# First norm from a token-major copy of x, first weights by halves, and a new order of the early pairs

## The chip, the cores and the metric

The kernel runs on one core of one Trainium2 chip. The metric is the device time of one execution, in microseconds (us). The engines are TensorE (PE), VectorE (DVE), ScalarE (ACT), GpSimd (POOL) and SyncE (SP), which here issues transfers. Each engine works through its own queue in order; semaphores tie the queues together.

## The reference

Two groups of requests, 512 and 256 tokens of 1024 features, go through two layers with shared weights. Cut to what matters:

```python
def rmsnorm(x, g):
    y = x32 * lax.rsqrt(jnp.mean(x32 * x32, axis=-1, keepdims=True) + EPS)
    return y.astype(x.dtype) * g

def swiglu(h, wg, wu, wd):
    return (jax.nn.silu(h @ wg) * (h @ wu)) @ wd

def even_layer(x, ...):
    x = x + 0.5 * swiglu(rmsnorm(x, f1_n), f1_g, f1_u, f1_d)
    x = x + mixer_ab(rmsnorm(x, mix_n), ...)
    x = x + 0.5 * swiglu(rmsnorm(x, f2_n), f2_g, f2_u, f2_d)
    return x
```

The odd layer is the same with `mixer_c` in the middle, and a last rmsnorm follows. The inner width of swiglu is 2816. All is float32.

## The kernel before, in words

**Phases.** The kernel runs l0f1, l0m, l0f2, l1f1, l1m, l1f2 (layer 0 and 1: first swiglu, mixer, second swiglu). x lies in SBUF feature-major, as 8 tiles of 128 features by 768 tokens; the tokens are cut into two halves of 384 columns (`HALVES`, `H` = 384).

**Products.** A float32 operand is split into a high part, rounded to fp32r (`...h`, `whi`), and the rest (`...l`, `wlo`). ACT makes the high part (`copy`, or an activation with the gain as its scale), DVE the low part by a subtraction. `mm3` then issues three fp32r matmuls: weights high by data high, weights high by data low, weights low by data high.

**One pair.** The inner width is worked in 11 pairs of 256 columns. For each pair, gate and up are computed by seven block products in place of eight, over blocks of x (feature half by token half) and blocks of the weights, with sums of blocks: `p1` (on b11, tiles x0 to x3 of the first token half), `p2` (on b21, x4 to x7 of the first half), then `p6` (t2), `p7` (t3), `p4` (n4), `p5` (t1) and `p3` (b22). t2, t3, t1 and n4 are sums of blocks of x, made with DVE combines (`tmp<-x,gains,tmp`). One block product is 12 matmuls of 128x128 by 384 columns. p1 and p2 of gate and up are 24 matmuls each.

**Early pairs.** For the first four pairs (`EARLY`) p1, p2 and the activation (`hidden(0, 0)`) run before anything else, in the order of the tuple `ORDER`; each number is the next step of that pair. They need only the first token half. p1 leaves its result in a PSUM bank, and ACT copies it to SBUF (`p`, L524) before p2 adds to the same bank. `product` takes a bank from one of two pools of four, `mm` and `aux`; in before, pair 3's bank X is in aux, the others' in mm. The weights come as `raw` tiles of 128x1024 (512 KB), four buffers; the five `whi` and five `wlo` buffers rotate.

**Norm.** The gain is multiplied in when the high and low parts are made; 1/rms, a number per token, is multiplied in behind the matmuls, in `hidden` (L508, L510). For a token half ACT squares the eight tiles (L216, L219), DVE sums them into `acc` (L220), three matmuls of `acc` by ones give the sums per token (`norm_tok`), a chain of 12 small DVE operations makes rsqrt, and `norm_spread` makes two diagonal matrices, of the high and the low part (`diag`, DVE L256 and ACT L254), which two matmuls by ones spread over all partitions. ACT copies the result to `acc` (L414). `hidden(0, 0)` needs that copy for the first half.

**Order.** PE's order is the order of the code (`manual_schedule`). The code of the norm and of the splits runs in generators (chains) that yield planned us: `DELAY0` sets how many planned us of PE's work lie ahead of the sum and of the spread for the first token half, and so where their matmuls stand in PE's queue. The order on the other engines is set by a scheduler, which `high_priority` and `issue_after` guide. SP issues its transfers in order, with up to eight in flight: each waits for the eighth before it. At the start they are x0 to x3 (first token half), two raws, x4 to x7, two raws, the second half of x, and the raws of pairs 2 and 3. Transfers for the later tables (`skew`) are put between raws.

## Time and profile before

| what | value |
|---|---|
| time, median of 3 runs | 2619.56 us (2619.34 to 2621.04) |
| time of the profiled execution | 2622.39 us |
| its span, first to last instruction | 2620.6 us |
| mean granted clock of PE | 0.991 |
| PE busy | 2559.6 us (98%) |
| DVE busy | 2257.1 us (86%) |
| ACT busy | 1369.9 us (52%) |
| first matmul | 9.11 us after the span's start |

Rows of the timeline give the start in us from the span's start, the length, the engine, the line, the operation, its tiles (out<-in) and its shape; brackets hold the idle time before it and what ended it. Neighbouring rows of an engine overlap a little, so what one costs is the distance of the starts. "ps_mm" and "ps_aux" are the two pools of PSUM. PE's matmuls are named by the data and the weights that they read: `ps_mm<-b110h,whi` is a matmul of p1.

### The profile page before, as it was taken

The numbers are of one execution on the slowest core, as the hardware profiler recorded it, in microseconds if no ns is written. First come the engines' busy times: TensorE is split into PE (matmuls) and PEld (weight loads), VectorE is DVE, ScalarE is ACT, GpSimd is POOL, SyncE is SP. The second block draws the span as 40 slices with busy tenths as digits, with TensorE's granted clock in tenths as the row PEclk, the third lists the DMA queues.
The fourth block names the chain that finished last, engine by engine and source line by source line (L and its number), as shares of the span: only waits on it lengthen the run. The fifth ranks groups of instructions, "written<-read, shape, count | busy, mean of one in ns | idle before, by whom it ended". The sixth has DMA issues, their size and how long they took to land.

```text
span 2620.6 us, 41173 instructions
## 1 busy us (share of the span) xinstructions
PE 2559.6 (98%) x15106; PEld 2493.7 (95%) x15106; DVE 2257.1 (86%) x4727; ACT 1369.9 (52%) x2858; POOL 90.4 (3%) x172
## 2 busy tenths in 40 slices
PE   7999999999999999999999999999999999999997
PEld 7999999988899999999999999989898999999997
DVE  8998899888779989889999888986777689888897
ACT  7554454555665545445654444554545465444543
POOL 0000000000100000000000000001122100000000
PEclk9999999999999999999999999999999999999999
DMA  5333222421222222222322222232221332222221
GB/s 169 114 110 97 80 66 65 156 73 45 81 77 97 97 74 72 75 79 73 98 80 89 73 66 80 81 115 60 63 63 42 104 102 85 81 71 75 73 69 69
DMA packets 83897, 218.72 MB, mean 83 GB/s; under 512 B 20208, under 2 KB 33008, under 8 KB 83696
## 3 DMA queue, kind: packets, MB, share of 16 engines
q1 hardware_dynamic: 83552, 216.08, 26.2%
q8 instruction: 118, 1.93, 0.3%
q14 instruction: 83, 0.68, 0.1%
q10 hardware_dynamic: 144, 0.03, 0.0%
HBM read 206.64 MB, written 15.07 MB: 85 GB/s over the span
## 4 chain that ended last, share of the span: by engine, by line
PE 86%; DVE 8%; ACT 3%; DMA 1%; issue 1%; POOL 0%; SPq 0%; DVEq 0%; ACTq 0%; POOLq 0%
PE ps_mm L140 54%; PE ps_aux L140 31%; DMA raw<-in_w 1%; DVE wlo L115 1%; PE ps_aux L144 1%; ACT p L913 1%; DVE xl L741 1%; DVE p L907 1%; DVE s L611 0%; DVE tl L197 0%; ACT whi L114 0%; DVE p L922 0%; ACT xh L740 0%; DVE x L708 0%; ACT sq L219 0%
## 5 line engine op out<-in xcount | busy, mean ns | idle before, releaser
L114 ACT CAST whi<-s 128x512 fp32r<-128x512 f32 x496 | 305.0, 620 | 409.6 <-DVE s L611 164.6
L114 ACT CAST whi<-raw 128x512 fp32r<-128x512 f32 x512 | 311.2, 618 | 238.0 <-PE ps_mm L140 104.2
L115 DVE TENSOR_TENSOR wlo<-s,whi 128x512 fp32r<-128x512 f32 x496 | 337.2, 685 | 55.5 <-ACT whi L114 53.2
L115 DVE TENSOR_TENSOR wlo<-raw,whi 128x512 fp32r<-128x512 f32 x494 | 336.7, 689 | 29.9 <-ACT whi L114 25.8
L140 PE MATMUL ps_mm<-db,whi 128*128 128x384 f32 x864 | 219.3, 334 | 0.5 <-DVE sg L508 0.5
L140 PE MATMUL ps_aux<-dt,whi 128*128 128x384 f32 x864 | 219.1, 334 | 0.0
L140 PEld LDWEIGHTS ps_mm<-db,whi 128*128 128x128 f32 x864 | 155.9, 188 | 0.8 <-DVE sg L508 0.8
L140 PEld LDWEIGHTS ps_aux<-dt,whi 128*128 128x128 f32 x864 | 156.0, 188 | 0.0
L140 PE MATMUL ps_mm<-xh,whi 128*128 128x512 f32 (+1 forms) x416 | 147.1, 354 | 4.0 <-ACT xh L740 4.0
L140 PE MATMUL ps_mm<-db,wlo 128*128 128x384 f32 x432 | 144.3, 334 | 0.0
L140 PE MATMUL ps_aux<-dt,wlo 128*128 128x384 f32 x432 | 144.3, 334 | 0.0
L140 PE MATMUL ps_mm<-xl,whi 128*128 128x512 f32 (+1 forms) x416 | 142.2, 342 | 1.1 <-DVE xl L741 1.1
L140 PE MATMUL ps_mm<-xh,wlo 128*128 128x512 f32 (+1 forms) x416 | 141.8, 341 | 0.0
L611 DVE TENSOR_TENSOR s<-raw 128x512 f32<-128x512 f32 x124 | 85.2, 687 | 23.7 <-DMA raw<-in_w 23.4
L611 DVE TENSOR_TENSOR s<-raw,raw 128x512 f32<-128x512 f32 x124 | 84.0, 686 | 21.1 <-DMA raw<-in_w 21.0
L499 DVE TENSOR_TENSOR u<-ps_aux,u 128x384 f32<-128x384 f32 x176 | 97.1, 552 | 3.9 <-PE ps_aux L140 3.5
L140 PE MATMUL ps_aux<-dh,whi 128*128 128x384 f32 x384 | 97.7, 335 | 0.6 <-DVE x L708 0.6
L913 ACT ACTIVATE p<-p,st 128x256 f32<-128x256 f32 (+3 forms) x144 | 68.9, 480 | 52.5 <-DVE st L911 52.4
L663 DVE TENSOR_TENSOR x<-ps_aux,x 128x384 f32<-128x384 f32 x160 | 84.8, 551 | 13.0 <-PE ps_aux L140 13.0
L140 PE MATMUL ps_mm<-oh,whi 128*128 128x384 f32 x256 | 89.6, 350 | 4.7 <-DVE x L890 4.0
L140 PEld LDWEIGHTS ps_mm<-xh,whi 128*128 128x128 f32 x416 | 80.3, 193 | 14.0 <-ACT xh L740 4.9
L140 PE MATMUL ps_mm<-ol,whi 128*128 128x384 f32 x256 | 87.9, 343 | 3.5 <-DVE ol L197 3.3
(488 smaller groups left out, 8049.3 us busy)
## 6 DMA issues: line engine op xcount, KB each, us to landing
raw<-in_w SPq DMA_DIRECT2D x350, 512.0 KB, 3.7
xdm<-x SPq DMA_DIRECT2D x16, 384.0 KB, 2.3
x<-in_x SPq DMA_DIRECT2D x16, 192.0 KB, 5.5
x<-xdm SPq DMA_DIRECT2D x8, 384.0 KB, 4.0
xold<-xdm SPq DMA_DIRECT2D x8, 384.0 KB, 3.0
out_y<-y SPq DMA_DIRECT2D x8, 384.0 KB, 2.4
tab<-skew SPq DMA_DIRECT2D x8, 256.0 KB, 5.5
raw<-in_w SPq DMA_DIRECT2D x8, 256.0 KB, 2.7
```

The costliest lines, as they stand in the source:

```text
L114: nc.scalar.copy(hi, src)
L115: (eng or nc.gpsimd).tensor_tensor(out=lo, in0=src, in1=hi.bitcast(F32), op=ALU.subtract)
L140: self.nc.tensor.matmul(out, lhsT=lhsT, rhs=rhs, start=start, stop=stop, **kw)
L144: self.nc.tensor.transpose(out, src, self.ident)
L499: nc.vector.tensor_tensor(out=t, in0=bank[key, n], in1=t, op=ALU.add)
L611: f = lambda o, x, y, op: self.nc.vector.tensor_tensor(out=o, in0=x, in1=y, op=op)
L663: nc.vector.tensor_tensor(out=o, in0=ps, in1=o, op=ALU.add)
L741: nc.vector.scalar_tensor_tensor(out=lo, in0=src, scalar=gain, in1=hi.bitcast(F32), op0=ALU.mult, op1=ALU.subtract)
L907: nc.vector.tensor_tensor_reduce(out=outs[i], in0=ps_list[i], in1=adds[i], scale=1.0, scalar=init[i], op0=ALU.add, op1=ALU.max, accum_out= ...
L913: nc.scalar.activation(outs[i], outs[i], AF.Exp, bias=nm[:, i : i + 1], accum_out=sm[:, i : i + 1])
```

## The change

In the first phase (l0f1) the sums of squares come from a second input, `xt`, x in token-major form (6 blocks of 128 tokens by 1024 features, 3.15 MB). It is loaded in 12 tiles of 128x512 (`tok_load`; eight buffers, the last four behind the first four squares). ACT squares each and sums along the row in the same instruction (`accum_out`); DVE adds the two halves and makes rsqrt for all 768 tokens in one chain of 6 columns. The diagonal matrices of the first half are made at once. The combines and splits of t3, n4, t1 and b22 are issued behind the last DVE piece of them (`rooted`). The squares stand behind the first two copies of p1, the second half of x behind the fourth.

The first weights are cut into halves of 256 KB: the first of them goes on ACT's queue, ahead of the gains, three behind x0 to x3, four behind x4 to x7. 22 matmuls of ones by ones (128 columns) stand ahead of the first product. POOL sets `ones` before `ident`.

In l0f1 and l1f1 (not in the phases that follow a mixer) the early pairs run in a new order: both steps of pair 2 before `hidden` of pairs 0 and 1. Pair 2's bank X is in aux there, pair 3's in mm. In these phases the second number of `DELAY0` is 13 in place of 11 (l0f1 has its own, `DELAYT`). `hidden(0, 0)` of l0f1 has high priority. The skew transfers begin four raws later.

SP's order at the start, before:
```order
1 L1459 DMA x_97<-in_x 128x384
2 L1459 DMA x_98<-in_x 128x384
3 L1459 DMA x_99<-in_x 128x384
4 L1459 DMA x_100<-in_x 128x384
5 L99 DMA raw_190<-in_w 128x1024
6 L99 DMA raw_192<-in_w 128x1024
7 L1459 DMA x_101<-in_x 128x384
```
and in the changed kernel (`first_87` to `first_90` are the weights of p1 and p2, gate and up of pair 0, then of pair 1):
```order
4 L1526 DMA x_106<-in_x 128x384
5 L104 DMA first_88<-in_w 128x512
6 L104 DMA first_89<-in_w 128x512
7 L104 DMA first_90<-in_w 128x512
8 L1526 DMA x_107<-in_x 128x384
9 L1526 DMA x_108<-in_x 128x384
10 L1526 DMA x_109<-in_x 128x384
11 L1526 DMA x_110<-in_x 128x384
12 L104 DMA first_87<-in_w 128x512
13 L104 DMA first_88<-in_w 128x512
14 L104 DMA first_89<-in_w 128x512
15 L104 DMA first_90<-in_w 128x512
```
The weights of p1 now stand as halves ahead of x4 to x7, those of p2 behind; behind these rows follow eight token tiles, then the second half of x, then the last four token tiles and the raws of pair 2. ACT's queue at the start, changed kernel:
```order
1 L104 DMA first_87<-in_w 128x512
2 L1504 ACT_TABLE_LOAD
3 L1504 COPY space<-ones 128x96
4 L1507 DMA gains<-in_gains 128x56
5 L119 CAST whi_257<-first_87 128x512
6 L399 ACTIVATE b110h<-x_103,gains 128x384
7 L119 CAST whi_276<-first_88 128x512
8 L399 ACTIVATE b111h<-x_104,gains 128x384
```
In before the gain rows of x0, x1 and x2 stood ahead of the first weight cast; now two casts stand among them.

ACT's queue later in l0f1, where before the copies p of pair 1 stand between splits:
```order
48 L196 CAST t22h<-tmp 128x384
49 L354 ACTIVATE t13h<-tmp,gains 128x384
50 L219 ACTIVATE sq<-x_104 128x384
51 L524 COPY p_343<-ps_mm_272 128x384
52 L196 CAST b221h<-tmp 128x384
53 L524 COPY p_385<-ps_mm_345 128x384
```
and in the changed kernel the copies p of pair 2 (those of pairs 0 and 1 stand further ahead, among the first squares):
```order
49 L119 CAST whi_618<-raw_593 128x512
50 L201 CAST b222h<-tmp 128x384
51 L296 ACTIVATE diag<-ident,yl 128x128 x2
52 L119 CAST whi_644<-raw_591 128x512
53 L296 ACTIVATE diag<-ident,yl 128x128
54 L201 CAST b223h<-tmp 128x384
55 L201 CAST t30h<-tmp 128x384
56 L201 CAST t31h<-tmp 128x384
57 L201 CAST t32h<-tmp 128x384
58 L569 COPY p_513<-ps_aux_492 128x384
59 L569 COPY p_535<-ps_aux_515 128x384
```
The copies that p2 of pair 2 needs now stand behind the diags and three casts of t3.

PE's queue at the start of l1f1, before (`ps_mm_13945` is the third block product, gate of pair 1):
```order
6811 L140 MATMUL ps_mm_13945<-b110h,whi_13946 128x384
6812 L140 MATMUL ps_mm_13945<-b110l,whi_13946 128x384
6813 L140 MATMUL ps_mm_13945<-b110h,wlo_13947 128x384
6814 L140 MATMUL ps_aux_13957<-diag,onesr 128x384 x2
6815 L140 MATMUL ps_mm_13945<-b111h,whi_13946 128x384
```
and in the changed kernel, where `ps_mm_13943` is that product and `ps_mm_13970` the one behind it:
```order
6820 L145 MATMUL ps_mm_13943<-b113h,whi_13944 128x384
6821 L145 MATMUL ps_mm_13943<-b113h,wlo_13945 128x384
6822 L145 MATMUL ps_mm_13970<-b110h,whi_13971 128x384
6823 L145 MATMUL ps_mm_13970<-b110l,whi_13971 128x384
6824 L145 MATMUL ps_mm_13970<-b110h,wlo_13972 128x384
6825 L145 MATMUL ps_aux_13990<-diag,onesr 128x384 x2
```
The spread of the norm stands one block product, 12 matmuls, further back.

The diff, cut to its core:

```diff
-DELAY0 = (7.0, 11.0)
+DELAY0 = (7.0, 13.0), (7.0, 11.0)
+WARM = 22
 DELAY1 = (26.0, 12.0)
+DELAYT = (0.0, 14.6)
+TOKW, TOKQ, SECOND = 2, (8, 0), 4
...
 EARLY = 4
-ORDER = (0, 1, 0, 1, 0, 2, 1, 3, 2, 3, 2, 3)
+ORDERS = (0, 1, 0, 1, 2, 2, 0, 1, 3, 2, 3, 3), (0, 1, 0, 1, 0, 2, 1, 3, 2, 3, 2, 3)
...
-        self.nc.sync.dma_start(raw, src)
-        if self.spare and i >= 16:
+        if raw is None:
+            raw = self.rawp.tile([P, nk * n], F32, tag="raw", name=f"raw{i}")
+        (eng or self.nc.sync).dma_start(raw, src)
+        if self.spare and i >= 20:
             self.spare.pop(0)()
...
+    def tok_load(self):
+
+        i = len(self.tok)
+        t = self.fw.tile([P, 512], F32, tag="s", name="tok", bufs=8)
+        self.nc.sync.dma_start(t, self.aps["xt"][i // 2, :, i % 2 * 512 : i % 2 * 512 + 512])
+        self.tok.append(t)
+
+    def tok_norm(self):
+
+        nc = self.nc
+        while len(self.copied) < TOKW:
+            yield 0.2
+        sm = self.sp.tile([P, 3, 6], F32, tag="sm", name="sm", bufs=3)
+        it = self.sp.tile([P, 6], I32, tag="smi", name="smi", bufs=2)
+        for i in range(12):
+            t = self.tok[i]
+            nc.scalar.activation(t, t, AF.Square, accum_out=sm[:, i % 2 * 2, i // 2 : i // 2 + 1])
+            if len(self.tok) < 12:
+                self.tok_load()
+        with self.tc.high_priority():
+            nc.vector.tensor_tensor(out=sm[:, 0, :], in0=sm[:, 0, :], in1=sm[:, 2, :], op=ALU.add)
+            self.rsqrt(sm[:, 1, :], sm[:, 0, :], 1.0 / D, sm[:, 0, :], sm[:, 2, :], it)
+            self.ry = sm[:, 1, :]
+            self.early = self.diags(self.ry[:, 0:3])
+        self.spawn(self.norm_rt(0, DELAYT))
+
     def norm_spread(self, y, pool=None):
 
-        nc = self.nc
+        return self.spread(self.diags(y, pool))
+
+    def spread(self, diags):
+
+        rb = self.psum(self.aux, "aux")
+        for i, diag in enumerate(diags):
+            self.mmul(rb[:, :H], self.onesr, diag, i == 0, i == 1)
+        return rb[:, :H]
+
+    def diags(self, y, pool=None):
+
+        nc = self.nc
+        res = []
         yh = self.sp.tile([P, 3], F32R, tag="yh", name="yh", bufs=2)
         yl = self.sp.tile([P, 3], F32, tag="yl", name="yl", bufs=2)
         nc.vector.tensor_copy(yh, y)
         nc.vector.tensor_tensor(out=yl, in0=y, in1=yh.bitcast(F32), op=ALU.subtract)
-        rb = self.psum(self.aux, "aux")
...
-            self.mmul(rb[:, :H], self.onesr, diag, i == 0, i == 1)
-        return rb[:, :H]
+                    ).ins
+            res.append(diag)
+        return res
 
     def rsqrt(self, y, src, scale, v, h, it):
...
-        with self.tc.high_priority():
-            y = self.norm_tok(self.acc, c0, c1)
+        if self.tok:
+            y = self.ry[:, 3 * h : 3 * h + 3]
+        else:
+            with self.tc.high_priority():
+                y = self.norm_tok(self.acc, c0, c1)
         yield d1
         with self.tc.high_priority():
-            self.r[h] = self.norm_spread(y)
+            self.r[h] = self.spread(self.early) if self.tok and not h else self.norm_spread(y)
 
...
+        fresh = bool(self.tok)
...
+                with self.tc.issue_after(self.rooted) if fresh else nullcontext():
...
-        for n in (1, 2):
-            while len(self.copied) < 2:
-                yield 0.2
...
+        while len(self.copied) < SECOND:
+            yield 0.2
+        with self.tc.issue_after(self.copied[SECOND - 1]):
+            for m in [i // 2 + (0 if i % 2 else 4) for i in range(KD)]:
+                self.feed(m, 1)
         self.half_done(1)
 
-    def norm_rt(self, h):
-
-        yield from self.norm_half(h, *(DELAY1 if h else DELAY0))
+    def norm_rt(self, h, delay=None):
+
+        yield from self.norm_half(h, *(delay or (DELAY1 if h else DELAY0[self.mixed])))
         c0, c1 = HALVES[h]
         self.nc.scalar.copy(self.acc[:, c0:c1], self.r[h])
         self.scales.add(h)
@@ -419,6 +462,7 @@
         if "work" not in self.guards:
             self.fw = self.open("work", self.other(self.guards["comb"][1]))
         rt, scales = self.acc, self.scales
...
+            fresh = bool(self.first)
...
-                    mm = key == "Y" or key == "X" and p != EARLY - 1
+                    mm = key == "Y" or key == "X" and p != EARLY - (1 if mixed else 2)
...
-                hidden(0, 0, bank["X", "gate"], bank["X", "up"])
+                with self.tc.high_priority() if fresh else nullcontext():
+                    hidden(0, 0, bank["X", "gate"], bank["X", "up"])
                 yield
...
-        for p in ORDER:
+        for p in ORDERS[mixed]:
             next(stages[p])
...
+        self.tok = []
+        self.mixed = False
...
-        self.norm_add(m, c0, c1)
+        if not self.tok:
+            self.norm_add(m, c0, c1)
...
+        self.mixed = True
...
-        self.cp.tile([P, 96], F32, tag="space", name="space")
+        space = self.cp.tile([P, 96], F32, tag="space", name="space")
+        todo = [KIND[p] for p in self.phases] + [("last", 6)]
...
+        self.ones = self.cp.tile([P, P], F32, tag="ones", name="ones")
+        self.onesr = self.cp.tile([P, P], F32R, tag="onesr", name="onesr")
+        if kind == "f":
+            pre = f"{self.phases[0][:2]}_ffn{self.phases[0][3]}_w_"
+            raws = [self.rawp.tile([P, KD * P], F32, tag="raw", name=f"first{i}") for i in range(4)]
+            self.first += [t.rearrange("p (k n) -> p k n", k=KD) for t in raws]
+
+            def first(i, k, eng=None):
+                name = pre + ("gate", "up")[i % 2]
+                self.raw(name, 4 * k, 4, i // 2 * 2 * P, P, raws[i][:, k * 512 : k * 512 + 512], eng)
+
+            first(0, 0, nc.scalar)
+        nc.gpsimd.memset(self.ones, 1.0)
+        nc.vector.tensor_copy(self.onesr, self.ones)
+        nc.scalar.copy(space, self.ones[:, :96])
         make_identity(nc, self.ident)
...
             self.mixer_tiles("right")
         self.norm_begin(todo[0])
+        self.mixed = False
+        if kind == "f":
+            ps = self.psum(self.aux, "aux")
+            for _ in range(WARM):
+                nc.tensor.matmul(ps[:, :P], lhsT=self.onesr, rhs=self.onesr, start=True, stop=True)
         for h, (c0, c1) in enumerate(HALVES):
             for m in range(KD):
                 nc.sync.dma_start(self.x[m][:, c0:c1], self.aps["x"][m, :, c0:c1])
-                if not (h and kind == "f"):
+                if kind == "f":
+                    if h == 0:
+                        self.feed(m, 0)
+                else:
                     self.final(m, c0, c1)
                 if h == 0 and m % 4 == 3 and kind == "f":
-                    pre = f"{self.phases[0][:2]}_ffn{self.phases[0][3]}"
-                    self.first += [self.raw(f"{pre}_w_{n}", 0, KD, m // 4 * 2 * P, P) for n in ("gate", "up")]
-            if h and kind == "f":
-                self.spawn(self.second())
-            elif kind in ("f", "last"):
+                    for i in range(4):
+                        if m > 4 or i:
+                            first(i, m // 4)
+            if kind == "f":
+                for _ in range(TOKQ[h]):
+                    self.tok_load()
+                if h:
+                    self.spawn(self.second())
+            elif kind == "last":
                 self.half_done(h)
             if kind == "last":
...
+    inp("xt", (T // P, P, D))
```

47 lines of the change are left out of this document (19 added, 28 removed).

## Prediction

> **What bounds the kernel now.** I read the shares of the whole span first, then what TensorE (PE) waits for at the start, then the stretches of the start, then PE's own timeline.
>
> The page's busy times:
> ```profile
> PE 2559.6 (98%) x15106; PEld 2493.7 (95%) x15106; DVE 2257.1 (86%) x4727; ACT 1369.9 (52%) x2858; POOL 90.4 (3%) x172
> ```
> PE's waits of 0 to 120 us (for what, us in total, times, longest):
> ```profile
> PE ps_mm L140 <- ACT whi L114: 9.1, 1, 9.1
> PE ps_mm L140 <- ACT p L524: 5.5, 1, 5.5
> PE ps_mm L140 <- DVE sg L508: 3.4, 1, 3.4
> ```
> PE is the bound, with 98%; a faster ACT or DVE helps only where PE waits for it. The change touches the start, where PE waits three times, 18 us together, and one later phase. The stretches of the start (busy us and count of each engine; then granted clock, DMA share, GB/s):
> ```profile
> 0.00:5.00 5.00, 0.00 (x0) 0.00 (x0) 0.23 (x1) 1.71 (x2) 1.28 (x8) 1.00 0.55 149
> 5.00:10.00 5.00, 0.89 (x3) 0.66 (x3) 3.14 (x6) 3.58 (x9) 0.00 (x0) 1.00 1.04 377
> 10.00:15.00 5.00, 5.00 (x17) 5.00 (x17) 4.99 (x11) 4.82 (x11) 0.00 (x0) 1.00 1.02 398
> 30.00:35.00 5.00, 4.02 (x13) 4.02 (x14) 5.00 (x14) 4.67 (x13) 0.00 (x0) 0.50 0.02 5
> 40.00:50.00 10.00, 8.62 (x41) 8.62 (x42) 9.98 (x21) 6.13 (x11) 0.00 (x0) 0.83 0.42 117
> 50.00:60.00 10.00, 10.00 (x61) 10.00 (x61) 9.13 (x23) 5.14 (x12) 0.00 (x0) 1.00 0.52 142
> ```
> DMA is full from 5 to 15 us, and VectorE (DVE) from 40 to 60. PE's timeline (start, length):
> ```profile
> 9.11 0.69 PE L140 MATMUL ps_mm<-b110h,whi 128*128 128x384 f32 x1 [9.11 <-ACT whi L114]
> ...
> 13.21 0.52 PE L140 MATMUL ps_mm<-b110h,whi 128*128 128x384 f32 x1
> 13.53 0.52 PE L140 MATMUL ps_mm<-b110l,whi 128*128 128x384 f32 x1
> ...
> 20.49 0.72 PE L140 MATMUL ps_aux<-ones,acc 128*128 128x1 f32 x6
> 21.08 0.42 PE L140 MATMUL ps_mm<-b210h,whi 128*128 128x384 f32 x1
> ...
> 30.98 0.69 PE L140 MATMUL ps_mm<-b210h,whi 128*128 128x384 f32 x1 [5.49 <-ACT p L524]
> ...
> 37.49 0.51 PE L140 MATMUL ps_aux<-diag,onesr 128*128 128x384 f32 x2
> 41.38 0.45 PE L140 MATMUL ps_mm<-b110h,whi 128*128 128x384 f32 x1 [3.38 <-DVE sg L508]
> ...
> 60.37 0.33 PE L140 MATMUL ps_mm<-t20h,whi 128*128 128x384 f32 x1
> ...
> 62.80 0.33 PE L140 MATMUL ps_mm<-t20h,wlo 128*128 128x384 f32 x1
> ```
> The early work is 192 matmuls, 24 for p1 and 24 for p2 of four pairs. p1 of two pairs is done at 20.49, p2 of both at 37.49, all 192 at 60.37. A matmul takes 0.32 us (13.21 to 13.53) at half clock and, with 14 of them from 60.37 to 62.80, 0.174 at full.
>
> **The change, by steps.** *First weights.* ScalarE (ACT) got its first weights here, after a wait:
> ```profile
> 8.44 0.62 ACT L114 CAST whi<-raw 128x512 fp32r<-128x512 f32 x1 [1.42 <-DMA raw<-in_w]
> ```
> By then 0.745 + 3.44 x 0.377 = 2.0 MB had moved, since up to eight transfers share the engines. Now ACT's second cast, of the half first_88, stands ahead of b111h. Among the first transfers are x0 to x3 and four halves, 1.84 MB: shared, 5 + (1.84 - 0.745) / 0.377 = 7.9 us. Served in order, first_88 is in after 1.31 MB, at 6.5. I take 8.4, as the 8.44 row, and keep 6.5 as the end.
>
> [...]
>
> Behind that cast ACT has two casts and the gain rows of x1 to x3. Its spacing, and that of its PSUM copies:
> ```profile
> 26.43 0.61 ACT L114 CAST whi<-raw 128x512 fp32r<-128x512 f32 x1
> 26.95 0.61 ACT L354 ACTIVATE t11h<-tmp,gains 128x384 fp32r<-128x384 f32 x1
> 27.47 0.60 ACT L354 ACTIVATE t12h<-tmp,gains 128x384 fp32r<-128x384 f32 x1
> ...
> 30.47 0.46 ACT L524 COPY p<-ps_mm 128x384 f32<-128x384 f32 x1
> 30.83 0.51 ACT L196 CAST b221h<-tmp 128x384 fp32r<-128x384 f32 x1
> ```
> Six steps of 0.52 from 8.4 end at 11.5, DVE's last split (b113l) about 1 us later, at 12.5, and its two matmuls at 12.9; before, the first product ended at 13.21. The other 36 matmuls of p1 take as long as before, 20.49 - 13.21 = 7.3: p1 of pairs 0 and 1 ends at 20.2.
>
> The 22 matmuls of ones (128 columns) lie in PE's idle 9.11 us. Bounds: a third of 0.32, or all of it, each: 2.4 to 7.0 us; either ends before the weights, so they cost nothing. Whether they raise the clock is open. If they do, six matmuls after 13.21 lose 0.146 less each, 0.9 us; I count nothing, because PE then idles again.
>
> [...]
>
> *The norm.* Removed: 16 squares on ACT and 14 sums on DVE; two groups of ones,acc matmuls (0.59 us each on PE). These groups of 0 to 62 us show them:
> ```profile
> L220 DVE TENSOR_TENSOR acc<-acc,sq 128x384 f32<-128x384 f32 x14 | 7.7, 549 | 0.0
> L219 ACT ACTIVATE sq<-x 128x384 f32<-128x384 f32 x14 | 6.9, 517 | 0.0
> ```
> Added: 12 accumulating squares of 512. Nearest rows:
> ```profile
> 569.56 0.60 ACT L913 ACTIVATE p<-p,st 128x384 f32<-128x384 f32 x1
> 570.07 0.18 ACT L913 ACTIVATION_READ_ACCUMULATOR p<-p,st 128x1 f32 x1
> 570.16 0.60 ACT L913 ACTIVATE p<-p,st 128x384 f32<-128x384 f32 x1
> ```
> One per 0.60 us against 0.52 for a plain one of 384, so accumulating adds 0.08: 0.60 for 512. Bounds 0.52 (nothing added) and 0.71 (the read's 0.18 in full).
>
> p2 of pairs 0 and 1 no longer waits 5.49: its copies stand ahead of the fifth square. 48 x 0.174 = 8.3, from 20.2 to 28.5 (before 37.49).
>
> Then PE needs pair 2's first cast (whi_493), which stands behind all twelve squares. The third product ends at 20.2 - 12 x 0.174 + 0.3 = 18.4; from there ACT has a cast 0.52, copy 0.37, three squares 1.8, copy 0.37, four squares 2.4, four gains 2.06, two casts 0.82, two squares 1.2, a gain 0.52, two squares 1.2, two casts 0.82, the cast 0.6: 12.7, to 31.1. PE idles 2.6 (24 matmuls of p1 follow, to 36).
>
> The squares' cover is DMA: 3.15 MB more on SP's queue, ahead of the second half of x and of the raws of pair 2. The last four token tiles wait for buffers that ACT's fourth square frees, at 21.1. Transfers of x took:
> ```profile
> DMA to landing us min/median/max: 2.5/5.5/6.7
> ```
> So they land at 23.6 to 27.8, and ACT needs the last at 29.1: 1.3 us or more to spare. The skew transfers go four raws later; nothing reads them in this phase, so no cost.
>
> p2 of pair 2 waits for two copies that stand in ACT's order behind t30h to t32h, which wait for DVE combines, held until the last diag. DVE's spacing:
> ```profile
> 24.09 0.15 DVE L276 SCALAR_TENSOR_TENSOR sm<-sm 128x3 f32<-128x3 f32 x1
> 24.16 0.68 DVE L115 TENSOR_TENSOR wlo<-raw,whi 128x512 fp32r<-128x512 f32 x1
> 24.76 0.15 DVE L274 TENSOR_TENSOR sm<-sm 128x3 f32<-128x3 f32 x1
> ...
> 38.78 0.61 DVE L362 SCALAR_TENSOR_TENSOR tmp<-x,gains,tmp 128x384 f32<-128x384 f32 x1
> 39.31 0.55 DVE L197 TENSOR_TENSOR t33l<-tmp,t33h 128x384 fp32r<-128x384 f32 x1
> 39.77 0.61 DVE L362 SCALAR_TENSOR_TENSOR tmp<-x,gains,tmp 128x384 f32<-128x384 f32 x1
> ```
> From 31.1: seven wlo of 0.60, nine small ones of 0.15, six diag pieces (0.2 each, an estimate between the 0.07 of a small one and 0.46 of a 384-wide one) and 0.3 for yh and yl: 7.1, to 38.2. Three combines of 0.53, a cast and a copy of 0.5 each: PE resumes at about 41. It stood idle some 5 us; after the 5.49 of before it ran at 0.50 clock (30:35), so I charge 13 matmuls x 0.146 = 1.9. At 41, 120 matmuls are done (96 before at 41.38). The other 72: 12.5 + 1.9 + 0.3 for the diag pair, to 55.8 against 60.37.
>
> That lead of 4.6 is not kept, since the t2 products wait for DVE next. From 38.2 to the lo part of the second t2 product DVE has 16 x 0.53 + 17 x 0.47 + 7 x 0.60 = 20.7, stretched by its busy share of 40 to 60 (19.11 of 20) to 21.7: 59.9, and the matmul at 60.1. Before it ran at 62.80. Of these 2.7, 0.3 goes on the next sums. **Start: 2.4 us.**
>
> *l1f1.* The new order and the later diag hold here too:
> ```profile
> 1258.78 0.34 PE L140 MATMUL ps_mm<-b110h,wlo 128*128 128x384 f32 x1
> 1260.50 0.61 PE L140 MATMUL ps_aux<-diag,onesr 128*128 128x384 f32 x2 [1.38 <-DVE diag L256]
> ```
> 12 matmuls of 0.174 now stand between: 2.1 us, more than the wait of 1.38. What waits for the diag (the scale, hidden) frees banks that pair 3 now needs, 48 matmuls later than pair 2 did. **1.4 us**, bounds 1.4 and -1.4 (the same wait at another place).
>
> Sum: 2.4 + 1.4 = 3.8. The profiled execution took 2622.39 us (span 2620.6 and 1.8 around it), 2.8 above the median of 2619.56; 2618.6 on its scale, 2615.8 on the median's: 2616.
>
> **The rivals.** *B, a larger gain.* The halves arrive in order, first_88 at 6.5, and the chain of ACT and DVE behind it moves 1.9 earlier as a whole; with the 0.9 of a clock that the ones raise it is 3.8 + 1.9 + 0.9 = 6.6: 2613. For it: the halves are smaller and stand ahead of x4 to x7. Against: 149 GB/s in 0:5, and eight transfers that share the engines.
>
> *C, nothing at the start.* DVE is full from 40 to 60 whatever PE does. If squares cost 0.71 (11 x 0.11 = 1.2) and the restart 1.3 more at half clock, the 2.4 is gone: 2618 with l1f1's gain, 2619.5 without.
>
> *D, slower.* ACT stops at a token tile that has not landed, and casts, copies, diags and PE stop with it. At 1.3 to 5.5 us of spare, the start's 3.8 and the 5.2 us that count as slower need the last tile some 12 us late, 17 us from issue to landing; beyond that each us costs one. At 18.5: 2626. The longest of x took 6.7, so it is unlikely.
>
> **How the numbers follow.** Within 0.2%, or 5.2 us, is about what a measurement of this kernel can tell from no change. The 2616 case (2614.4 to 2617.5 by itself, all same) 0.47; B 0.36, faster; C 0.09, same; D 0.08, slower. Bounds: low, squares at 0.52 (+0.9), casts at 6.5 (+1.9), the ones' 0.9 and no half clock after the gap (+1.9): 3.8 + 5.6 = 9.4, 2610.2, of which I cut the last tenths, since all four must meet; high, squares at 0.71 (-1.2), a second stretch at half clock (14 matmuls x 0.146 = 2.0), and nothing in l1f1: 2.4 - 3.2 = -0.8, 2620.4. D stays outside: 2610.5 to 2620.5.
>
> **What would show it.** ACT's second weight cast near 8.4 (B: 6.5); no wait on p before PE's 49th matmul; a wait on whi near 28 and one on p from 36 to 41, half clock behind it; the second t2 product near 60; no diag wait in l1f1. Wrong if DVE is not late at t2 (then up to 4.6 at the start), or if a token tile stops ACT.

## The result, and the profile after

The changed kernel takes 2612.8 us (median of 20 runs, 2609.66 to 2618.85); the kernel before, in 20 runs beside it, 2616.9 (2614.03 to 2622.6). The ratio is 0.9983, with a 95% interval of 0.9977 to 0.9990: 4.4 us less, between 2.6 and 6.0. Forecast were 3.8 less and 2616; in the longer series before itself is at 2616.9, and 2612.8 lies inside the range. The absolute time is the one that rival B had (2613), under the 2614.4 to 2617.5 of the 2616 case: before itself ran 2.7 us under the three runs that the forecast started from. It is the difference, 4.4, that stands near the 3.8 of that case; B's 6.6 lies outside its interval.

The profiled execution of the changed kernel has a span of 2612.3 us, 8.3 under that of before. That is more than the runs show, and the reason is below: part of the pair's difference is scatter between two executions. The page's busy times:

```profile
PE 2561.3 (98%) x15116; PEld 2493.1 (95%) x15116; DVE 2249.0 (86%) x4701; ACT 1370.3 (52%) x2867; POOL 90.4 (3%) x172
```

DVE has 8.1 us less work (2257.1 before), most of it the 14 sums of squares that are gone. PE's waits of 0 to 120 us:

```profile
PE ps_aux L145 <- ACT p L569: 4.4, 1, 4.4
PE ps_aux L145 <- ACT whi L119: 2.4, 1, 2.4
PE ps_aux L1523 <- DVE onesr L1503: 1.3, 1, 1.3
PE ps_mm L145 <- ACT b111h L399: 1.2, 1, 1.2
```

The waits on p and on sg that cost 5.5 and 3.4 us before are gone, and two others stand in their place, on the first cast of pair 2 (2.4) and on the copies of pair 2 (4.4). The stretches of the start (busy us and count of each engine, then granted clock, DMA share, GB/s):

```profile
5.00:10.00 5.00, 3.77 (x12) 2.52 (x11) 3.21 (x6) 3.26 (x7) 0.79 (x1) 1.00 1.00 339
20.00:25.00 5.00, 5.00 (x31) 5.00 (x30) 1.29 (x3) 5.00 (x16) 0.00 (x0) 1.00 1.07 398
25.00:30.00 5.00, 2.88 (x17) 2.55 (x15) 4.40 (x13) 5.00 (x14) 0.00 (x0) 1.00 0.96 386
30.00:35.00 5.00, 4.50 (x16) 4.03 (x17) 4.49 (x14) 5.00 (x11) 0.00 (x0) 0.66 0.09 17
40.00:50.00 10.00, 8.95 (x43) 8.83 (x44) 10.00 (x22) 8.88 (x20) 0.00 (x0) 0.83 0.35 103
50.00:60.00 10.00, 9.49 (x53) 8.85 (x53) 10.00 (x20) 4.90 (x10) 0.00 (x0) 1.00 0.24 38
```

PE is now busy from 20 to 25 without a gap, ACT is full from 20 to 30, where most of the squares stand, and DVE is full from 40 to 60. From 30 to 35 the granted clock is 0.66: the wait of 2.4 us on pair 2's first cast, too, was followed by a stretch at half clock (30.6 to 34.0). On PE's timeline:

```profile
1.25 4.96 PE L1523 MATMUL ps_aux<-onesr 128*128 128x128 f32 x22 [1.25 <-DVE onesr L1503]
8.54 0.69 PE L145 MATMUL ps_mm<-b111h,whi 128*128 128x384 f32 x1 [1.18 <-ACT b111h L399]
30.32 0.45 PE L145 MATMUL ps_aux<-b110h,whi 128*128 128x384 f32 x1 [2.44 <-ACT whi L119]
41.05 0.69 PE L145 MATMUL ps_aux<-b210h,whi 128*128 128x384 f32 x1 [4.41 <-ACT p L569]
55.54 0.33 PE L145 MATMUL ps_mm<-t20h,whi 128*128 128x384 f32 x1
58.91 0.44 PE L145 MATMUL ps_mm<-t20h,wlo 128*128 128x384 f32 x1 [0.27 <-DVE wlo L120]
1260.69 0.51 PE L145 MATMUL ps_aux<-diag,onesr 128*128 128x384 f32 x2
```

The early 192 matmuls end at 55.5 (60.4 before), the second t2 product waits a little for DVE and runs at 58.91 (62.80 before), and in l1f1 the spread by ones no longer waits. On ACT the casts and copies that these rest on:

```profile
7.35 0.62 ACT L119 CAST whi<-first 128x512 fp32r<-128x512 f32 x1 [1.71 <-DMA first<-in_w]
29.65 0.61 ACT L119 CAST whi<-raw 128x512 fp32r<-128x512 f32 x1
40.52 0.85 ACT L569 COPY p<-ps_aux 128x384 f32<-128x384 f32 x2
```

### The profile page after: what moved, and what is told of

It reads as the page before. It is cut to its first block, busy times and chain, and to the rows that moved or that the text cites. A ratio compares the mean times of both kernels' runs of the same rounds, so it can differ in the third digit from the quotient of the medians.

```text
span 2612.3 us, 41192 instructions
## 1 busy us (share of the span) xinstructions
PE 2561.3 (98%) x15116; PEld 2493.1 (95%) x15116; DVE 2249.0 (86%) x4701; ACT 1370.3 (52%) x2867; POOL 90.4 (3%) x172
## 4 chain that ended last, share of the span: by engine, by line
PE 86%; DVE 9%; ACT 2%; DMA 1%; issue 1%; SPq 0%; DVEq 0%; ACTq 0%
PE ps_mm L145 53%; PE ps_aux L145 32%; DVE wlo L120 1%; PE ps_aux L149 1%; DMA raw<-in_w 1%; ACT p L963 1%; DVE xl L790 1%; DVE p L957 0%; DVE tl L202 0%; DVE ol L202 0%; DVE p L972 0%; ACT xh L789 0%; DMA x<-in_x 0%; DVE tmp L407 0%; DVE s L659 0%
## 5 line engine op out<-in xcount | busy, mean ns | idle before, releaser
L120 DVE TENSOR_TENSOR wlo<-s,whi 128x512 fp32r<-128x512 f32 x496 | 336.6, 683 | 53.7 <-ACT whi L119 51.2
L120 DVE TENSOR_TENSOR wlo<-raw,whi 128x512 fp32r<-128x512 f32 x486 | 330.1, 687 | 24.8 <-ACT whi L119 19.0
L711 DVE TENSOR_TENSOR x<-ps_mm,x 128x384 f32<-128x384 f32 x160 | 86.0, 550 | 5.9 <-PE ps_mm L145 5.6
```

Of the source, the lines that this page charges most:

```text
L120: (eng or nc.gpsimd).tensor_tensor(out=lo, in0=src, in1=hi.bitcast(F32), op=ALU.subtract)
L711: nc.vector.tensor_tensor(out=o, in0=ps, in1=o, op=ALU.add)
```

## The experiments

Each kernel was timed beside runs of the kernel before on the same chip. Ratios are to those runs, with 95% intervals; 0.001 is 2.6 us. A difference between the ratios of two kernels is good to some 3 us to either side. The granted clock of a run goes with its time: the changed kernel's runs took 2615.5 us on the mean of three at 0.990 and 2609.8 on the mean of three at 0.993, 1.9 us for each 0.001. Its mean clock over twenty runs is 0.9914, and that of before 0.991. The traces add where a difference stands. "Matmul 767" below is the 768th matmul, counted from 0, that reads a block of x (b, t or n in its name), a point at 186 us in the changed kernel where every kernel here has done the same products.

### The kernel before, once more

How far do two executions of one program differ? The edit is none.

> The kernel before once more, for its trace: how far its start and its l1f1 differ between executions. Theory (starts differ by the landing of the first transfers and by the clock): the same waits as before, matmul 767 of the first phase within 2.5 us of 189.7, and the ratio within 0.1% of 1.

The ratio is 1.0001 (0.9992 to 1.0010). Its span was 2611.7 us, against 2620.6 in the first profile, with the same three waits at the start:

```profile
PE ps_mm L140 <- ACT whi L114: 8.1, 1, 8.1
PE ps_mm L140 <- ACT p L524: 5.5, 1, 5.5
PE ps_mm L140 <- DVE sg L508: 3.4, 1, 3.4
```

The first wait is 1.0 us shorter, matmul 767 comes at 188.3 in place of 189.7, and l1f1 and later parts make up the rest. The early matmuls end at 59.1 (60.4 in the first profile), and the second t2 product's low part runs at 61.54 (62.80). So one pair of profiles can't settle a difference of 4 us; what follows goes by the ratios, and by traces where a wait has a name.

### The two places apart

The parts of l0f1 alone, with l1f1 as before:

```diff
-DELAY0 = (7.0, 13.0), (7.0, 11.0)
+DELAY0 = (7.0, 11.0), (7.0, 11.0)
...
-        mixed = bool(self.unfed)
+        mixed = bool(self.unfed) or not self.tok
```

> The parts of l0f1 alone; l1f1 keeps the old order and the old delay. Theory (the start gives 2.4 us or a little more, l1f1 1.4 by its one wait on the diag): the wait of 1.4 us on the diag in l1f1 is back, all else at the start is as in the changed kernel, and the time lies 2.4 to 3.7 us under before, 1.4 over the changed kernel. Rival (the gain is the start's alone and the wait in l1f1 only moves): the same time as the changed kernel, about 4 us under before.

And the change of l1f1 alone in the kernel before:

```diff
-DELAY0 = (7.0, 11.0)
+DELAY0 = (7.0, 13.0), (7.0, 11.0)
...
+        mixed = bool(self.unfed) or bool(self.first)
...
-                    mm = key == "Y" or key == "X" and p != EARLY - 1
+                    mm = key == "Y" or key == "X" and p != EARLY - (1 if mixed else 2)
...
-        for p in ORDER:
+        for p in ORDERS[mixed]:
```

> The kernel before with the new order, the swapped banks and the delay of 13 in l1f1 alone. Theory: no wait on the diag at the start of l1f1, none in its place, and 1.4 us under before. Rival: a wait of the same size at another place of l1f1 and no change.

The start alone has 0.9982 (0.9973 to 0.9991), l1f1 alone 0.9987 (0.9979 to 0.9996). Both are gains, and the sum of the two, 8 us, is more than the 4.4 of the whole; the intervals, some 2.3 us to either side, just allow it, so the runs don't settle the shares. The traces give that of l1f1 closer. With the start alone the wait in l1f1 stands as before, and with l1f1 alone there is none:

```profile
1262.26 0.62 PE L145 MATMUL ps_aux<-diag,onesr 128*128 128x384 f32 x2 [1.38 <-DVE diag L298]
```

```profile
1262.67 0.51 PE L140 MATMUL ps_aux<-diag,onesr 128*128 128x384 f32 x2
```

Over the stretch from 781 us, well ahead of l1f1, to 1395, behind its early pairs, PE took 616.05 us in the second profile of before and 616.05 with the start alone, but 613.89 in the changed kernel and 614.65 with l1f1 alone: 1.4 to 2.2 us for l1f1. (The first profile of before had 617.75.) Four kernels further down that also have the new order in l1f1 took 613.5 to 614.1 there. Nothing took the place of the wait, and the rival that it only moves falls. For the start, matmul 767 stands at 189.7, 188.3 and 187.7 in the three traces that have the start of before, and at 186.0 and 185.6 in the two that have the new one: 2.7 us between the means, 1.6 to 4.1 by single traces. The next but one experiment, whose start differs from the changed one by a queue alone, has 188.6; counted in, its trace leaves 1.8 us between the means.

The traces do not show that this lead lasts. The matmul at 781.1 us in the changed kernel stands at 781.6, 780.1 and 782.7 in the three traces with the start of before, and at 783.0 with the start alone. Between matmul 767 and that point the two traces of before have 6.8 us at half clock, the changed kernel 13.7 and the start alone 20.5. It is not a matter of the start only, since l1f1 alone has 13.7 there with the old start, and the kernel with 188.6 has 6.8 with the new one. That the start's gain is one of the whole kernel rests on the ratios.

### Without the ones

```diff
-WARM = 22
+WARM = 0
```

> The changed kernel without the 22 matmuls of ones. Theory (the ones only raise the clock of the first products): the first 48 real matmuls take up to 0.9 us longer, ACT's chain behind the third product moves by as much, and the time rises by 0.5 to 0.9 us. Rival 1 (they are worth nothing, since DVE sets the time of the second t2 product): the same time within 0.2 us, the t2 product at 58.9. Rival 2 (much of the gain is theirs): 2 us or more.

The ratio is 0.9981 (0.9972 to 0.9990), the same as with them. The first product ends 0.14 us later and p1 of two pairs 0.3 later, at 19.5 in place of 19.2; matmul 767 is at 186.3 against 186.0 and 185.6. By these traces the 22 matmuls of ones are worth 0.3 to 0.7 us, less than single traces differ; no run here shows that they are worth anything. The first product begins 0.24 us sooner without them (5.77 against 6.01).

### The first half of weights on SP's queue

```diff
-            first(0, 0, nc.scalar)
...
-                        if m > 4 or i:
-                            first(i, m // 4)
+                        first(i, m // 4)
```

> The changed kernel with the first half of weights on SP's queue, with the other three, in place of ACT's; the gains stay on ACT's. Theory (the queue that issues it makes little of the time; what counts is the bytes ahead): first_88, the one that ACT's second cast waits for, lands within 0.5 us of 7.3, the first product ends within 0.5 us of 12.5, and the time is the same within 0.5 us. Rival (one more issue ahead of it on SP, 0.47 us, and a later first_87 shift the whole chain): 0.5 to 1.5 us over the changed kernel.

0.9982 (0.9973 to 0.9991): no difference that the runs show. ACT takes the four casts in one piece from 7.63 us:

```profile
7.63 2.56 ACT L119 CAST whi<-first 128x512 fp32r<-128x512 f32 x4
```

and the first product's last matmul starts at 12.07 against 12.45. Its first matmul comes 2.3 us later than in the changed kernel, whose row stands second:

```profile
8.30 0.69 PE L145 MATMUL ps_mm<-b110h,whi 128*128 128x384 f32 x1 [2.09 <-ACT whi L119]
6.01 0.63 PE L145 MATMUL ps_mm<-b110h,whi 128*128 128x384 f32 x1
```

The half that it waits for was issued at 2.60 and landed at 7.61, against 0.73 and 4.23 on ACT's queue. So the queue, and with it the place ahead of x0 to x3, did bring that half 3.4 us sooner; the product as a whole did not end sooner for it. In this trace matmul 767 comes at 188.6, 2.6 us later than in the changed kernel, with a wait on pair 2's first cast of 3.8 us in place of 2.4 and 6.8 us at half clock twice; the runs, which agree with the changed kernel to 0.0001, don't carry that over, so I take it for one execution's.

### Half of the squares left out

Six of the twelve squares on ACT are left out, and the half sum is counted twice (the norm is that of half the features).

```diff
-            nc.scalar.activation(t, t, AF.Square, accum_out=sm[:, i % 2 * 2, i // 2 : i // 2 + 1])
+            if i % 2 == 0:
+                nc.scalar.activation(t, t, AF.Square, accum_out=sm[:, 0, i // 2 : i // 2 + 1])
```

> The changed kernel with six of the twelve token squares left out (the sums of the other half of the features are left out and the half that is there counted twice); all twelve tiles are still loaded. ACT has 3.7 us less ahead of the first cast of pair 2. Theory (DVE, not ACT, sets the time of the second t2 product): PE's wait of 2.4 us on that cast goes, the wait on the copies of pair 2 stays within 1 us of 4.4 or grows, and the time falls by 0 to 1.5 us against the changed kernel. Rival (the squares on ACT are on the path): 3 us or more are gained.

The ratio is 0.9994 (0.9985 to 1.0003), no faster than the changed kernel and, if anything, slower; the rival of 3 us and more falls, and the theory's 0 to 1.5 us don't show in the runs either. Its runs had a mean clock of 0.9900, 0.0014 under the changed kernel's, which goes with some 2.7 us; in the trace matmul 767 comes at 185.1, 1 us sooner than in the changed kernel. PE's waits of 0 to 160 us, the largest three:

```profile
PE ps_mm L145 <- ACT whi L119: 2.1, 1, 2.1
PE ps_aux L145 <- ACT p L570: 1.7, 1, 1.7
PE ps_aux L145 <- ACT whi L119: 1.7, 1, 1.7
```

The wait on the copies went from 4.4 to 1.7 and that on pair 2's first cast from 2.4 to 1.7, the early matmuls end 4 us sooner, at 51.4, and then PE waits 2.1 us before the t2 products, whose second comes at 58.1, 0.8 sooner than 58.9. DVE is busy 20.00 of 20 us from 40 to 60. I had expected the cast's wait to go and the copies' to stay; the first went down by 0.7 only, and the second fell by 2.7.

### The copies of pair 2 first

The splits behind the diag are also held behind the copies of pair 2. They then stand ahead of t30h in ACT's order, and hidden of pairs 0 and 1 ahead of most combines in DVE's.

```diff
         fresh = bool(self.tok)
+        while fresh and len(self.copied) < 6:
+            yield 0.2
...
-                with self.tc.issue_after(self.rooted) if fresh else nullcontext():
+                with self.tc.issue_after(self.rooted) if fresh else nullcontext(), self.tc.issue_after(self.copied[5]) if fresh else nullcontext():
```

> The changed kernel with the splits of t3, n4, t1 and b22 held behind the copies of pair 2 as well as behind the diag, so that these copies stand ahead of t30h in ACT's queue and hidden of pairs 0 and 1 ahead of most combines in DVE's. Theory (DVE sets the end of the start; the stall of 4.4 us on the copies is mostly hidden behind it): the stall falls under 1.5 us, and the second t2 product moves by 0 to 2.1 us only, the four t1 splits of 0.53 that now stand behind it. Rival (PE's stalls count in full): 4.4 us and the half clock behind it, 1.9, so 5 to 6 us faster than the changed kernel.

The stall on the copies is down to 0.9 us, and the kernel is slower: 1.0007 (0.9998 to 1.0015), 6 us over the changed one. PE's waits of 56 to 165 us (the changed kernel has two there, of 0.3 and 0.2):

```profile
PE ps_mm L145 <- ACT whi L119: 4.1, 1, 4.1
PE ps_aux L145 <- DVE wlo L120: 2.2, 1, 2.2
PE ps_mm L145 <- DVE wlo L120: 0.9, 1, 0.9
```

PE finished its early matmuls at 51.2, 4 us sooner, and then waited 4.1 for a cast that itself waits for a sum on DVE; the second t2 product came at 60.7, and two more waits followed. The clock was at half from 55.3 to 62.2, around the end of the first wait, and from 127.0 to 130.4, behind the wait of 2.2; the one of 0.9 brought no such stretch. Taking PE's largest stall away did not pay, since PE stood still for the same work of DVE a little later. That it got worse by as much as 6 us neither theory had said: the new order put DVE's work for the t2 products further back. Some 2 of the 6 us go with the clock, 0.9903 on the mean of the runs.

### The old order with the token norm

```diff
-        for p in ORDERS[mixed]:
+        for p in ORDERS[mixed or bool(self.tok)]:
...
-                    mm = key == "Y" or key == "X" and p != EARLY - (1 if mixed else 2)
+                    mm = key == "Y" or key == "X" and p != EARLY - (1 if mixed or self.tok else 2)
```

> The changed kernel with the old order of the early pairs and the old banks in l0f1 alone; token norm, halves and ones stay, l1f1 has the new order. Theory: with the old order PE needs hidden of pair 0, and so the whole norm, after 96 matmuls, at about 29 us, while the scale is ready at 45: a wait of 12 us or more on sg in place of the two of 2.4 and 4.4, the second t2 product no earlier than 60, and 2 to 6 us over the changed kernel. Rival (DVE sets the end whatever PE waits for): within 1 us of the changed kernel.

1.0006 (0.9997 to 1.0015): the gain is gone, l1f1's too. PE's largest waits:

```profile
PE ps_aux L145 <- DVE diag L298: 8.3, 1, 8.3
PE ps_mm L145 <- DVE sg L553: 5.2, 1, 5.2
```

13.5 us in place of 6.8. The token tiles come last of the first 8.4 MB, so the scale is later than before (PE goes on behind `sg` at 43.4, against 41.4 and 40.1 in the two traces of before), and only the new order has matmuls to put in front of it. Of the 6.0 us between this kernel and the changed one some 4 go with the clock, 0.9892 on the mean.

### The old norm with the new order

```diff
-            self.spawn(self.tok_norm())
...
                     if h == 0:
                         self.feed(m, 0)
+                        self.norm_add(m, 0, H)
...
             if kind == "f":
-                for _ in range(TOKQ[h]):
-                    self.tok_load()
                 if h:
                     self.spawn(self.second())
+                else:
+                    self.half_done(0)
```

(In `second` the sums of the second half stand again behind the feeds.)

> Halves, ones and the new order stay; the first norm is made as before: feature-major squares on ACT, 14 sums on DVE, matmuls of ones, and no token tiles. Theory (DVE's work at the start sets its end; the token norm takes 7.7 us of sums and a second chain of small operations from it): PE's waits of 2.4 and 4.4 us change their names, the second t2 product comes 2 to 4 us later than in the changed kernel, and the time rises by as much, to about before. Rival (the new order and the halves are the gain): within 1 us of the changed kernel.

1.0000 (0.9989 to 1.0010): here, too, the gain is gone. But not where I had it: the second t2 product came at 57.1, sooner than in the changed kernel, and at 73.0 PE was 0.3 us ahead of it. The loss comes later: it is 0.4 us behind at 82.9 and 3.4 at 106.6, and still 3.4 at matmul 767. PE's waits of 56 to 165 us, and the stretch from 80 to 110:

```profile
PE ps_mm L145 <- DVE wlo L120: 2.0, 4, 0.8
PE ps_mm L145 <- ACT whi L119: 1.5, 1, 1.5
...
80.00:110.00 30.00, 27.07 (x151) 25.67 (x150) 29.63 (x56) 16.93 (x35) 0.00 (x0) 1.00 0.42 139
```

DVE is full (29.63 of 30), PE is not (27.07). Of the 3.5 us of waits, 2.0 are on low parts and 1.5 on a cast. In the changed kernel that stretch reads:

```profile
80.00:110.00 30.00, 30.00 (x175) 29.87 (x174) 29.71 (x57) 18.07 (x37) 0.00 (x0) 1.00 0.36 125
```

### The old norm without its sums

The same kernel, with the 14 sums of squares on DVE left out in the first norm; the norm then holds the first square of each half alone. The squares on ACT stay.

```diff
             nc.scalar.activation(sq, self.x[m][:, a:b], AF.Square)
-            nc.vector.tensor_tensor(out=self.acc[:, a:b], in0=self.acc[:, a:b], in1=sq, op=ALU.add)
+            if not self.first_norm:
+                nc.vector.tensor_tensor(out=self.acc[:, a:b], in0=self.acc[:, a:b], in1=sq, op=ALU.add)
```

> The kernel with the old norm under the new order and halves, with the 14 sums of squares on DVE left out in the first norm (the squares of the other feature tiles do not reach the norm). Theory (the token norm's worth is the 7.7 us of DVE that it takes away): PE's waits on DVE's low parts between 80 and 106 us, 3.5 us, go, and the time falls by 3 to 5 us against the old norm with its sums, to that of the changed kernel. Rival (it is worth something by the earlier scale, or by what it does to ACT): within 1.5 us of the old norm with its sums.

0.9971 (0.9960 to 0.9983), 7.6 us under the old norm with its sums, good to some 4 us, since this kernel has six runs. The 14 sums take 7.7 us by the length of their rows and 6.6 by the 0.47 us at which such rows follow each other. The traces agree: from the 48th matmul, the end of p1 of two pairs, to matmul 767 PE takes 164.0 us without the sums and 170.3 with them, 6.3 less. Its waits of 56 to 165 us:

```profile
PE ps_mm L145 <- DVE wlo L120: 0.8, 1, 0.8
```

So under this order the sums cost about what they take of DVE's time, and leaving them out gives no less than the token norm does (4.4 us between that kernel and the old norm). The size is over what I expected (3 to 5).

### More work for DVE

Eight additions of 384 columns that nothing reads stand behind the diag in the changed kernel.

```diff
+                if fresh and n in ("t3", "n4"):
+                    with self.tc.issue_after(self.rooted):
+                        extra = self.np_.tile([P, H], F32, tag="nt", name="extra", bufs=3)
+                        self.nc.vector.tensor_tensor(out=extra, in0=self.x[k][:, c0:c1], in1=self.x[k + 4][:, c0:c1], op=ALU.add)
```

> The changed kernel with eight more additions of 384 on DVE behind the diag, 8 x 0.47 = 3.8 us; nothing reads their result. Theory (DVE is full from 40 to 110 us and PE's lead hangs on it): PE waits on DVE's low parts or sums by 110 us, and the time rises by 2.5 to 4 us. Rival (PE is the bound, DVE has room): 0 to 1 us.

1.0013 (1.0003 to 1.0023), 7.8 us over the changed kernel, good to some 3, for 3.8 us of DVE. PE's waits of 56 to 165 us:

```profile
PE ps_mm L145 <- DVE wlo L120: 2.6, 3, 1.5
PE ps_mm L145 <- ACT whi L119: 1.9, 1, 1.9
PE ps_aux L145 <- DVE wlo L120: 0.4, 1, 0.4
...
40.00:60.00 20.00, 15.74 (x74) 15.42 (x74) 19.17 (x41) 11.59 (x25) 0.00 (x0) 0.83 0.38 88
60.00:80.00 20.00, 18.81 (x97) 18.21 (x98) 16.39 (x29) 8.79 (x19) 0.00 (x0) 0.91 0.36 132
```

The wait on the copies, too, went from 4.4 to 5.9 us. The clock is at half from 42.2 to 49.0, twice as long as in the changed kernel, and once more from 62.6 to 66.0. Up to matmul 767, which comes at 196.5, 10.4 us later, PE stood idle 14.9 us in place of 9.0 from its first product on, and it had 6.8 us more at half clock, which by an estimate cost up to half of that (in the traces of before and of the changed kernel a matmul took 0.32 us at half clock and 0.174 at full): 5.9 and 3.4 are most of the 10.4. The runs say the same in the mean: their clock is 0.9895 against 0.9914, which goes with 3.6 us, and 4.2 are left for the 3.8 of DVE.

### Combines ahead of the diag

An attempt at a better version: between 20 and 30 us DVE is idle for 4.3 us (1.29 and 4.40 busy of 5 each). Only the splits of t3 and n4 stay behind the diag; their combines may run before it.

```diff
+                if n == "t3":
+                    t = self.etile("tmp")
+                    self.combine(t, self.x[k][:, c0:c1], -1, k, self.tmp[k + 4])
+                elif n == "n4":
+                    t = self.tmp["t2", k]
+                    self.combine(t, self.x[k + 4][:, a0:a1], 1, k + 4, t)
                 with self.tc.issue_after(self.rooted) if fresh else nullcontext():
...
+                    elif n in ("t3", "n4"):
+                        self.split(*self.b[n][k], t)
```

> The changed kernel with only the splits of t3 and n4 behind the diag; their eight combines, 4.2 us of DVE, may run before it, where DVE stands idle for some 5 us between 20 and 35 us. Theory: DVE's work behind the diag falls by up to 4 us, the diag and the scale come up to 3 us later, and the time lies 0 to 2 us under the changed kernel. Rival (the hold has its reason: the scale comes too late, and PE waits for it): 1 to 4 us over it.

1.0016 (1.0007 to 1.0025), 8.6 us over the changed kernel: the rival, and more. PE's waits of 0 to 165 us, the largest:

```profile
PE ps_aux L145 <- ACT whi L119: 4.1, 2, 2.6
PE ps_aux L145 <- DVE diag L298: 2.8, 1, 2.8
PE ps_mm L145 <- ACT whi L119: 2.0, 1, 2.0
```

The inputs of the combines come only when x's second half has passed ACT, so they ran among the small operations of the norm (27.9 to 41.2 us) and not in the idle stretch, the first diag came at 41.9 in place of 36.0, and PE waited for it. The mean clock is 0.9895 here too. The hold behind the diag has its reason. No kernel here that does all the work beats the changed one; those without the ones, with the first half on SP's queue and with the start alone are level with it.

## Why the prediction was right, and where it was off

*The first weights.* ACT's second cast ran at 7.35, between the ends of 6.5 and 8.4 that I had; the first product's last matmul at 12.45 and done at 12.8 (12.9 predicted). The case of transfers served in order (6.5) did not come. That 12.8 is so near 12.9 is in part luck: the cast came 1.0 sooner than I took, and DVE's last split of b11 ended 1.0 sooner (11.5), but PE, at 0.32 us a matmul, was itself the last by then. The halves and the ones together end p1 no sooner than before does by itself: its 48th matmul starts at 20.3, 19.1 and 18.8 in the three traces with the old start, and at 19.2 and 18.8 in the two with the new one. With ACT's and with SP's queue the ratio is the same to 0.0001, although the traces have first_87 issued 1.9 us earlier on ACT's (0.73 against 2.60) and landed 3.4 earlier (4.23 against 7.61).

*The ones.* Predicted 0 to 0.9 us, counted as nothing. Measured 0.3 to 0.7 in the traces, nothing in the runs. They filled 1.25 to 6.21 us on PE's timeline, 4.96 us, and the matmuls behind them still followed each other at 0.32 us from 11.5 to 13.4. In the trace without them the 24 matmuls from 15.3 to 19.5 run at the full 0.173 us each, so they are not what raises the clock behind the first product.

*The squares, at 0.60 us.* Right: they follow each other every 0.61 (20.44, 21.07, 21.68, 22.30 on ACT's timeline). The first cast of pair 2 ran at 29.65 (30.5 by the sum, since it was to end at 31.1), PE's wait was 2.4 (2.6). What the sum left out is the half clock behind that wait, although it charged one for the next: p1 of pair 2 took from 30.3 to 36.5, 6.2 us in place of 24 x 0.174 = 4.2. PE began 0.8 sooner, and 31.1 + 4.2 is 35.3, not the 36 of the prediction; these two hid most of it, which is luck. It cost nothing here, since PE then waited for the copies anyway. The last token tile landed at 26.45, ACT took it at 28.23: 1.8 us to spare (1.3 or more), and the slower case did not come.

*The copies of pair 2.* Right: PE stood 4.4 us and went on at 41.05 (some 5 us, at about 41), the clock at one half behind it (40.9 to 44.3). The early matmuls ended at 55.5 (55.8).

*The lead that is not kept.* Right in kind: PE left the early matmuls 4.8 us ahead of before and kept 3.9 at the second t2 product (3.6 and 2.6 against the second profile of before); the waits there are 0.24 us for a cast and 0.27 for DVE. Sized at 60.1, it came at 58.9. The term that was off is DVE's work of 20.7 us, stretched to 21.7 and started at 38.2. On DVE's timeline the first combine behind the diags started at 38.40 and the low part was done at 58.85, 20.4 us. The stretch of 1.0 did not come, because DVE had no idle time between (20.00 of 20 from 40 to 60), and four of the 16 operations counted at 0.53 followed each other at 0.47.

*Start 2.4, l1f1 1.4.* Measured by traces 2.7 at matmul 767 (1.6 to 4.1; 1.8 with the trace that has SP's queue) and 1.4 to 2.2; together 4.4 by the runs (2.6 to 6.0), against 3.8. The agreement of the sums is better than the scatter of single traces lets one claim. The diag's wait of 1.38 went as a whole.

*What I had not seen.* I let the bookkeeping stop at the second t2 product. The runs show that work on DVE counts up to 110 us: with the old norm PE was as far at 73 us as in the changed kernel, and lost 3.7 us, most of it in waits on low parts and a cast, by 107. The sums, 6.6 to 7.7 us of DVE, which in my sum only made DVE's queue shorter before t2, are what the start's gain rests on, together with the new order. The new order without the token norm, and the token norm without the new order, each give nothing (1.0000 and 1.0006, l1f1's change included); together 0.9983. Two rivals that I didn't write down, that either part alone is the gain, are thereby excluded within their intervals.

What stays open: where in the run the kernel with more work on DVE gets its lower clock (0.9895 against 0.9914), and why the shares of the two places add up to more than the whole by the ratios, for which the intervals are just wide enough. No run leaves out the halves of the first weights, the later second half of x or the later skew transfers alone; the traces give the first of them no gain by the end of p1, and the other two are untested.

## What to carry to other kernels

At the start of a program follow the queue of the second-busiest engine as far as its backlog reaches, not only to the next wait of the busiest: here DVE was full for 70 us (69.06 busy from 40 to 110), and what paid at the start took work from it and let PE have other work meanwhile. A stall that is removed without taking work from the engine behind it can come back a few microseconds later and dearer, as with the copies of pair 2, where a new wait of 4.1 us came with 6.8 us at half clock. A difference of a few us needs the runs: single traces of one program differed by more than the change is worth (8.9 us against 4.4). And a pair of parts (a cheaper norm that comes later, an order that can wait for it) may be worth something only together, so test each alone before judging either.

## What the runs showed of the hardware that was not expected

Two executions of one program differed by 8.9 us in the profiled span (2620.6 and 2611.7), though the runs' medians agreed within 0.0001 in ratio. 1.4 us of it stood at the start, 1.7 about l1f1's early pairs, and 2.9 in the 23 us behind 2113, where the first ran at half clock from 2128 to 2135 and the second not at all; the other 2.9 are spread over the rest. Behind the start the first profile has half clock at 582, 684, 1756 to 1766, 2101 and 2128 to 2135 us, the second at 581, 683 and 1751 to 1765. In the trace of the changed kernel and in the first of before, the stretches that end before the kernel does are 3.4, 6.8, 10.2 or 13.7 us long, and all their edges within one trace lie on one grid of 3.413 us from the first rise of the clock (13.6 us in the changed kernel, 15.4 in before) to the end of the kernel. A short idle stretch was followed by half clock in one execution and not in others: behind a wait of PE of 1.4 to 1.5 us near 630 us the changed kernel ran at half clock (631.4 to 634.8), and neither trace of before did. The two traces of before have different sums, 37.5 and 30.7 us of half clock between the first rise and 2600 us.
